# Storing groups 5 and 6 in partition-strided pieces, some of them from GpSimd

## The chip, the cores and the metric

The kernel runs on one core of one Trainium2 chip. The metric is the device time of the core in microseconds, the median of repeated executions: 132.0 us before the change (3 runs, 132.0 to 132.01).

## The reference

A batched matrix product of 32 pairs, in float32:

```python
# x: (32, 256, 512)   y: (32, 512, 384)   result: (32, 256, 384)
np.einsum('bij,bjk->bik', x, y).astype(np.float32)
```

The inputs are 16.8 MB and 25.2 MB, the output 12.6 MB. The kernel rounds the inputs to float16 for TensorE and accumulates in float32.

## The kernel before

The 32 products are done in N = 8 groups of Q = 4. A group's four products fill the 128 partitions together: each product has PQ = 32 of them, so partition p belongs to product p // 32 of the group. For x a partition holds R = 8 rows of i (a run of 16 KB in memory), for y T = 16 rows of j (24 KB), for the output 8 rows of i (12 KB).

SyncE issues all DMAs. Groups 0 and 1 are loaded at once (L75), the later ones each when the buffer of two groups earlier has been rounded (L98 to L102). GpSimd rounds x and y to float16 (L126, L136), VectorE transposes x in blocks of 32x32 (L156), TensorE multiplies four products at a time, each on 32 rows of its array (L217), into eight PSUM banks: four for the half e = 0 of the output rows, four for e = 1. ScalarE and VectorE copy the banks into `o_sb` (L165), which holds the output of all eight groups. TensorE starts a half only when the copies of the half before last have been made (`take(s_act)`, `take(s_dve)`), and it increments `s_pe` as it finishes chunks and banks; so the value of `s_pe` that says that chunk 0 of the last half of a group is done also says that all groups before that one are in `o_sb`.

The output leaves in three stores, all by `store(first, last)` (L93), each a DMA over 128 partitions:

- groups 0 to 4 (`JOINED` = 5) when TensorE has done chunk 0 of the last half of group 5 (L103, L104);
- groups 5 and 6 when it has done chunk 0 of the last half of group 7 (L105, L106). A partition gives two runs of 12 KB, one for each group;
- group 7 when the last copies have been made (L107 to L109).

All DMAs of SyncE stand in one queue, in the order of issue. After the last issue SyncE tells GpSimd through `s_sp` (L110) and waits until the three stores have landed (L111; each landing adds 16 to `s_out`). GpSimd, when its casts are done, waits for `s_sp` and clears the kernel's semaphores (L144, L145).

Of the kernel before, what the change touches and what calls it, by code (L numbers as in the profile page):

```python
# [10 lines left out]
P = 128  # L11
Q = 4
NE = 2
STEP = 4
STRAIGHT = 2
JOINED = 5
# [3 lines left out]
def kernel(  # L20
# [6 lines left out]
    nc = tc.nc  # L27
# [4 lines left out]
    PQ = P // Q  # L32
    R = I // PQ
# [3 lines left out]
    N = B // Q  # L37
    NC = T // STEP

    def sbuf(name, shape, dtype):  # L40
        return nc.alloc_sbuf_tensor(name, shape, dtype).ap()
# [3 lines left out]
    o_sb = sbuf("o_sb", [P, N, NE, H, K], F32)  # L45
# [6 lines left out]
    s_x = [nc.alloc_semaphore(f"s_x{n}") for n in range(N)]  # L52
    s_y = [nc.alloc_semaphore(f"s_y{n}") for n in range(N)]
    s_xt = nc.alloc_semaphore("s_xt")
    s_yr = nc.alloc_semaphore("s_yr")
    s_cast = nc.alloc_semaphore("s_cast")
    s_free = nc.alloc_semaphore("s_free")
    s_act = nc.alloc_semaphore("s_act")
    s_dve = nc.alloc_semaphore("s_dve")
    s_pe = nc.alloc_semaphore("s_pe")  # L60
    s_sp = nc.alloc_semaphore("s_sp")
    s_out = nc.alloc_semaphore("s_out")
    mine = s_x + s_y + [s_xt, s_yr, s_cast, s_free, s_act, s_dve, s_pe, s_sp]
    nums = sorted(s.num for s in mine)
    assert nums == list(range(nums[0], nums[-1] + 1)) and s_out.num == nums[-1] + 1

# [21 lines left out]
    def chunk_done(n, e, a):  # L88
        return (n * NE + e) * MARKS + (a + 1 if a < NC - 1 else MARKS)

    sp = nc.sync

    def store(first, last):  # L93
        groups = out[first * Q : last * Q].rearrange("(n g) (s f) k -> (g s) n f k", g=Q, s=PQ)
        src = o_sb[:, first:last].rearrange("p n e h k -> p n (e h) k")
        sp.dma_start(out=groups, in_=src).then_inc(s_out, 16)

    for n in range(2, N):  # L98
# [3 lines left out]
        load_y(n)  # L102
    sp.wait_ge(s_pe, chunk_done(JOINED, NE - 1, 0))  # L103
    store(0, JOINED)  # L104
    sp.wait_ge(s_pe, chunk_done(N - 1, NE - 1, 0))  # L105
    store(JOINED, N - 1)  # L106
    sp.wait_ge(s_act, NE)  # L107
    sp.wait_ge(s_dve, NE)
    store(N - 1, N)  # L109
    sp.sem_inc(s_sp, 1)  # L110
    sp.wait_op(s_out, 16 * 3, "sem-ge").then_inc(s_out, -16 * 3)  # L111

    def pieces(n):
        w = 1 if n in (0, N - 2, N - 1) else 2
        return [(a, a + w) for a in range(0, NC, w)]

    po = nc.gpsimd

    def round_x(n):
        po.wait_ge(s_x[n], 16)
        for e in range(NE):
            if n:
                po.wait_ge(s_free, max(2 * n - 2 + e, 1))
            po.tensor_copy(  # L126
                x_r[:, e], x_sb[n % 2][:, e * H : (e + 1) * H]
            ).then_inc(s_cast, 1)

    def round_y(n):  # L130
        po.wait_ge(s_y[n], 16)
        for a, b in pieces(n):
            if n:
                po.wait_ge(s_pe, chunk_done(n - 1, NE - 1, b - 1))
            s = slice(a * STEP, b * STEP)
            ins = po.tensor_copy(y_r[:, s], y_sb[n % 2][:, s])  # L136
            ins.then_inc(s_yr, b - a if b < NC else b - a + NC)
# [3 lines left out]
    for n in range(1, N):  # L141
        round_x(n)
        round_y(n)
    po.wait_ge(s_sp, 1)  # L144
    po.sem_clear(range(nums[0], nums[-1] + 1))  # L145

# [84 lines left out]
    with te.Fori(0, N):  # L231
        with te.Fori(0, NE) as e:
            take(s_act)
            take(s_dve)
            for t in range(T):
# [3 lines left out]
                for g in range(Q):  # L239
                    s = slice(g * PQ, (g + 1) * PQ)  # L240
# [40 lines left out]
```

## Time and profile before

| | |
|---|---|
| median of 3 runs | 132.0 us |
| the profiled execution | 132.13 us |
| its span, first to last instruction | 130.8 us |
| granted TensorE clock, mean | 0.823 |
| bytes read from HBM, written to it | 41.94 MB, 12.58 MB |

The transfers, by what is issued, with the size of one and the median time from its issue to its landing:

```profile
## 6 DMA issues: line engine op xcount, KB each, us to landing
y_sb<-in_y_dram SPq DMA_DIRECT2D x8, 3072.0 KB, 16.8
x_sb<-in_x_dram SPq DMA_DIRECT2D x8, 2048.0 KB, 17.0
out_dram<-o_sb SPq DMA_DIRECT2D x1, 7680.0 KB, 33.9
out_dram<-o_sb SPq DMA_DIRECT2D x1, 3072.0 KB, 17.3
out_dram<-o_sb SPq DMA_DIRECT2D x1, 1536.0 KB, 11.5
```

How to read it: a core has 16 DMA engines, and a DMA is done by several of them, each with its own packets; a transfer that is issued while others are still queued lands long after its issue. PE is TensorE's matmul, PEld its weight load, DVE VectorE, ACT ScalarE, POOL GpSimd, SP SyncE; a "q" behind a name is the engine's sequencer. Rows of stretches give the stretch, its length, busy time and count for PE, PEld, DVE, ACT and POOL, the granted clock, the busy share of the DMA engines and their GB/s, where a packet is counted in the stretch in which it starts. Rows of waits give who waited for whom, the sum in us, how often, and the longest.

### The profile page before, as it was taken

To read this page: it belongs to the slowest core of one execution; us is meant where nothing else is said; L and a number is where in the kernel's file an instruction comes from. 1 tells how busy PE (TensorE), PEld (TensorE's weight loads), DVE (VectorE), ACT (ScalarE), POOL (GpSimd) and SP (SyncE) were. 2 spreads that over 40 slices of the span, in tenths; PEclk is the share of its full clock that TensorE was granted. 3 is DMA by queue.
4 is the path that set the end of the run, shared out by engine and by line. 5 is a ranking of instruction groups with operands and counts; after the bars stand their busy time and mean duration, and the time that the engine had idled before them with its cause. 6 is when DMAs were issued, how large, how long until landed. Compare 5 with 4: busy or idle time off the path is not lost. (4 is left out here: it accounts for less than half of the span.)

```text
span 130.8 us, 3199 instructions
## 1 busy us (share of the span) xinstructions
PE 61.4 (47%) x1024; PEld 46.7 (36%) x1024; DVE 82.7 (63%) x144; ACT 84.1 (64%) x178; POOL 74.2 (57%) x42
## 2 busy tenths in 40 slices
PE   0000009910992589089329905980975499100000
PEld 0000009800991566046129604970953236000000
DVE  0000036899379999985997997599999957920000
ACT  0400000599659989993998899399999957994000
POOL 0006991199929965992899459758973970000000
PEclk9999999995589689977986985599599959965555
DMA  5999999999999999999999999999999999999995
GB/s 120 451 396 441 421 431 451 443 408 428 451 413 421 438 443 401 436 436 443 423 458 398 443 408 466 398 418 436 463 398 408 427 438 425 436 428 421 425 440 248
DMA packets 3379, 54.55 MB, mean 417 GB/s; under 512 B 304, under 2 KB 304, under 8 KB 304
## 3 DMA queue, kind: packets, MB, share of 16 engines
q1 hardware_dynamic: 3376, 54.53, 98.1%
q14 instruction: 3, 0.02, 0.0%
HBM read 41.94 MB, written 12.58 MB: 417 GB/s over the span
## 5 line engine op out<-in xcount | busy, mean ns | idle before, releaser
L165 ACT COPY o_sb<-o_ps (+1 forms) x176 | 82.6, 469 | 31.7 <-PE o_ps L217 29.6
L217 PE MATMUL o_ps<-y_r,xt_sb 32*128 32x384 f16 x1024 | 61.4, 384 | 50.4 <-PEq L214 49.5
L217 PEld LDWEIGHTS o_ps<-y_r,xt_sb 32*128 32x128 f16 x1024 | 46.7, 107 | 64.6 <-issue 56.8
L156 DVE STREAM_TRANSPOSE xt_sb<-x_r 128x256 f32<-128x256 f32 x64 | 38.1, 626 | 30.9 <-POOL x_r L126 18.4
L136 POOL CAST y_r<-y_sb 128x1536 f16<-128x1536 f32 (+1 forms) x22 | 44.3, 2049 | 15.8 <-DMA y_sb<-in_y_dram 15.3
L165 DVE COPY o_sb<-o_ps 32x384 f32 (+1 forms) x80 | 44.6, 557 | 1.6
L126 POOL CAST x_r<-x_sb 128x2048 f16<-128x2048 f32 x16 | 30.2, 1893 | 16.8 <-DVE o_sb L165 12.1
L202 ACT ACT_TABLE_LOAD x1 | 1.3, 1283 | 3.4 <-PEq L78 3.4
L265 POOL MEMSET const-float32-0.0<- 128x1 f32 x1 | 0.1, 98 | 0.2 <-issue 0.2
L202 ACT COPY spare<-const-float32-0.0 1x1 f32<-1x1 f32 x1 | 0.2, 190 | 0.0
L265 POOL MEMSET const-bfloat16-1.0<- 128x1 bf16 x1 | 0.1, 101 | 0.0
L265 POOL MEMSET const-uint8-127<- 128x1 uint8 x1 | 0.1, 101 | 0.0
L265 POOL MEMSET const-float32-1.0<- 128x1 f32 x1 | 0.1, 98 | 0.0
## 6 DMA issues: line engine op xcount, KB each, us to landing
y_sb<-in_y_dram SPq DMA_DIRECT2D x8, 3072.0 KB, 16.8
x_sb<-in_x_dram SPq DMA_DIRECT2D x8, 2048.0 KB, 17.0
out_dram<-o_sb SPq DMA_DIRECT2D x1, 7680.0 KB, 33.9
out_dram<-o_sb SPq DMA_DIRECT2D x1, 3072.0 KB, 17.3
out_dram<-o_sb SPq DMA_DIRECT2D x1, 1536.0 KB, 11.5
```

What stands on the lines that cost most here:

```text
L126: po.tensor_copy(x_r[:, e], x_sb[n % 2][:, e * H : (e + 1) * H]).then_inc(s_cast, 1)
L136: ins = po.tensor_copy(y_r[:, s], y_sb[n % 2][:, s])
L156: v.transpose(xt_w[:, w], words[:, e, w]).then_inc(s_xt, 1)
L165: ins = copy(o_sb[g * PQ : (g + 1) * PQ, n, e, h], o_ps[h * PQ : (h + 1) * PQ, e * Q + g, :K],)
L202: a_.copy(spare, nc.const_aps.tensor(0.0, [1, 1], F32))
L217: return te.add_instruction(mybir.InstMatmult(name=nc.get_next_instruction_name(), start_tensor_calc=start, stop_tensor_calc=stop, tile_si ...
L265: nc = _bacc.Bacc("TRN2", target_bir_lowering=False, num_devices=1)
```

## The change

The store of groups 5 and 6 is replaced by seven DMAs. A new function `store_rows(eng, sem, first, step, rows, f0, f1)` stores, for both groups, the output rows f0 to f1 (of the 8) of the partitions first, first + step and so on. SyncE stores the even partitions (64), then 1, 5, 9, ... (32), then 3, 11, 19, ... (16). Of the remaining 16 partitions, 7, 15, ..., 127, it stores rows 1 to 7 (10.5 KB in each group) of the first four in one DMA and of the fifth, 39, in another. GpSimd stores row 0 (1.5 KB in each group) of these five, and then all 8 rows of the other eleven, 47 to 127, after the same mark of TensorE and its last casts. GpSimd's two DMAs count on a semaphore of their own, `s_few`, for which SyncE waits after it has issued the last store and before it tells GpSimd to clear the semaphores. `s_out` now counts seven DMAs of SyncE: groups 0 to 4, these five, and group 7.

```diff
+    s_few = nc.alloc_semaphore("s_few")
...
+    def store_rows(eng, sem, first, step, rows, f0=0, f1=R):
+        dst = out[JOINED * Q : (N - 1) * Q].rearrange("(n g) (s f) k -> (g s) n f k", g=Q, s=PQ)
+        src = o_sb[:, JOINED : N - 1].rearrange("p n e h k -> p n (e h) k")
+        p = slice(first, first + (rows - 1) * step + 1, step)
+        eng.dma_start(out=dst[p, :, f0:f1], in_=src[p, :, f0:f1]).then_inc(sem, 16)
...
     sp.wait_ge(s_pe, chunk_done(N - 1, NE - 1, 0))
-    store(JOINED, N - 1)
+    store_rows(sp, s_out, 0, 2, P // 2)
+    store_rows(sp, s_out, 1, 4, P // 4)
+    store_rows(sp, s_out, 3, 8, P // 8)
+    store_rows(sp, s_out, 7, 8, 4, 1)
+    store_rows(sp, s_out, 39, 8, 1, 1)
     sp.wait_ge(s_act, NE)
     sp.wait_ge(s_dve, NE)
     store(N - 1, N)
+    sp.wait_ge(s_few, 16 * 2)
     sp.sem_inc(s_sp, 1)
-    sp.wait_op(s_out, 16 * 3, "sem-ge").then_inc(s_out, -16 * 3)
+    sp.wait_op(s_out, 16 * 7, "sem-ge").then_inc(s_out, -16 * 7)
...
+    po.wait_ge(s_pe, chunk_done(N - 1, NE - 1, 0))
+    store_rows(po, s_few, 7, 8, 5, 0, 1)
+    store_rows(po, s_few, 47, 8, 11)
     po.wait_ge(s_sp, 1)
     po.sem_clear(range(nums[0], nums[-1] + 1))
```

More of the change, by code (lines that the diff above doesn't have):

```diff
@@ L61 @@
     s_sp = nc.alloc_semaphore("s_sp")
+    s_few = nc.alloc_semaphore("s_few")
     s_out = nc.alloc_semaphore("s_out")
-    mine = s_x + s_y + [s_xt, s_yr, s_cast, s_free, s_act, s_dve, s_pe, s_sp]
+    mine = s_x + s_y + [s_xt, s_yr, s_cast, s_free, s_act, s_dve, s_pe, s_sp, s_few]
     nums = sorted(s.num for s in mine)
```

## The prediction

> **What bounds the kernel now.** I read the page first, for the busy shares, then the work by stretches of time, then what SyncE's queue waited for, and last the transfers in the final microseconds, since those decide how much there is to win.
>
> ```profile
> span 130.8 us, 3199 instructions
> PE 61.4 (47%) x1024; PEld 46.7 (36%) x1024; DVE 82.7 (63%) x144; ACT 84.1 (64%) x178; POOL 74.2 (57%) x42
> DMA packets 3379, 54.55 MB, mean 417 GB/s; under 512 B 304, under 2 KB 304, under 8 KB 304
> q1 hardware_dynamic: 3376, 54.53, 98.1%
> ```
>
> No compute engine is busy for two thirds of the span; the 16 DMA engines are busy for 98.1% of it, with one queue. The chain of waits is no help: it ends at the last copy, as it follows instructions and not transfers. The stretches show it better.
>
> ```profile
> 0.00:1.70 1.70, 0.00 (x0) 0.00 (x0) 0.00 (x0) 0.00 (x0) 0.20 (x4) 1.00 0.00 0
> ...
> 106.00:119.40 13.40, 5.74 (x96) 3.04 (x95) 7.15 (x13) 10.77 (x23) 1.03 (x1) 0.75 1.01 431
> 119.40:126.30 6.90, 0.00 (x0) 0.00 (x0) 0.00 (x0) 0.00 (x0) 0.00 (x0) 0.50 1.01 433
> 126.30:128.90 2.60, 0.00 (x0) 0.00 (x0) 0.00 (x0) 0.00 (x0) 0.00 (x0) 0.50 0.98 421
> ```
>
> After the start-up of 1.7 us the engines never run dry, and from 119.4 us on nothing computes: the kernel ends when its bytes are out. At 433 GB/s one of 16 engines moves 27.06 KB (of 1,000 bytes) per us; I use that below. So an edit of the last stores can pay in one way only: by spreading the same bytes over the engines so that the last one ends sooner. How unevenly they end now is seen in the completions. The 304 packets under 512 B on the page are 16 for each of the 19 DMAs: each engine closes its part of a DMA with one, so such packets count the engines that finish the last store.
>
> In 129.0 to 129.6 us, then 129.6 to 130.0, then 130.0 to 130.8:
>
> ```profile
> DMA packets 22, 0.16 MB, mean 266 GB/s; under 512 B 9, under 2 KB 9, under 8 KB 9
> ...
> DMA packets 7, 0.01 MB, mean 31 GB/s; under 512 B 6, under 2 KB 6, under 8 KB 6
> ...
> DMA packets 1, 0.00 MB, mean 0 GB/s; under 512 B 1, under 2 KB 1, under 8 KB 1
> ```
>
> Nine engines finish before 129.6, six more before 130.0, one alone after that. The median engine is near 129.55. To place the late one:
>
> ```profile
> 129.25:129.50 0.25, 0.00 (x0) 0.00 (x0) 0.00 (x0) 0.00 (x0) 0.00 (x0) 0.50 0.82 344
> 129.50:129.80 0.30, 0.00 (x0) 0.00 (x0) 0.00 (x0) 0.00 (x0) 0.00 (x0) 0.50 0.01 0
> 129.80:130.20 0.40, 0.00 (x0) 0.00 (x0) 0.00 (x0) 0.00 (x0) 0.00 (x0) 0.50 0.08 31
> ```
>
> A packet is counted where it starts: 31 GB/s over 0.40 us is 12.4 KB, one packet of 12,288 B, begun after 129.80 when the other 15 engines had begun their last before 129.50. It takes 12,288 / 27.06 KB = 0.45 us, so the late engine ends at 130.25 or later; I take 130.3. The next ends before 129.95 (begun by 129.50, plus 0.45). The late engine alone thus costs about 0.35 us. That is the prize, 0.27% of the time.
>
> **The change, part by part.** It takes the store of groups 5 and 6 apart.
>
> ```profile
> SPq L96 <- PE o_ps L217: 23.5, 1, 23.5
> SPq L111 <- SPq L111: 11.1, 1, 11.1
> SPq L108 <- DVE o_sb L165: 5.0, 1, 5.0
> SPq L96 <- ACT o_sb L165: 4.0, 1, 4.0
> ...
> 109.82 9.80 SPq L96 DMA_DIRECT2D out_dram<-o_sb  x2
> ...
> 101.33 5.70 POOL L136 CAST y_r<-y_sb 128x1536 f16<-128x1536 f32 x4 [2.18 <-DMA y_sb<-in_y_dram]
> ...
> L96 SPq DMA_DIRECT2D out_dram<-o_sb x3: 345/390/403, 85.9 to 119.3; - x3
> ...
> DMA to landing us min/median/max: 11.5/17.3/33.9
> L145 POOLq EVENT_SEMAPHORE_RANGE_CLEAR  x1: 163/163/163, 119.7 to 119.7; - x1
> ```
>
> *Issue on SyncE.* One issue at 109.82 becomes five, at 0.345 to 0.403 us each: up to 4 x 0.40 = 1.6 us more, done by about 111.8. Behind them stand only the waits for the last copies (5.0 and 4.0 us) and the last store, issued at 119.3: 7 us to spare. The engines meanwhile work on the store of groups 0 to 4 (issued at 85.9, landed 33.9 us later, at 119.8). Cost nothing; without that cover, 1.6 us.
>
> *Issue on GpSimd.* It finishes its casts at 101.33 + 5.70 = 107.03, waits for the same mark of TensorE and issues two DMAs. No row shows a DMA issued by GpSimd. The bounds: 0.35 us each as on SyncE below; above, its idle time to the end, 130.8 - 109.8 = 21 us, for the two together. Its transfers go ahead in the 20 us in which other packets fill the engines. I take nothing, as even ten times SyncE's issue (2 x 4 us) ends at 118. If the cover were gone, the largest row, 24,576 B, would take 0.91 us at the end.
>
> *The new wait.* SyncE waits for GpSimd's transfers after the last store is issued. Behind it stand the increment of s_sp and the final wait; for s_sp only GpSimd's clear of the semaphores waits (0.163 us, at 119.7 now). Nothing as long as GpSimd's rows land before about 130.6, at most 0.2 us beyond.
>
> *The bytes.* The total stays. In the old store each engine had 3,072 KB / 16 = 196,608 B. Of the new ones the three sets of 64, 32 and 16 rows divide by 16: 172,032 B to each engine. The remaining 16 rows come in portions: SyncE sends 4 of 21,504 B and 1 of 21,504 B, GpSimd 5 of 3,072 B and 11 of 24,576 B. If every row of a DMA falls to an engine of its own and GpSimd's five and eleven fall to different ones, eleven engines get 24,576 B and four 21,504 + 3,072 = 24,576 B, all as before. The fifth row's large part is a DMA by itself: nothing puts it on the engine that has that row's small part. So one engine is lighter by 21,504 B, 0.79 us, and one is heavier by that, or two by 0.40 us each. The trace names no engine of a packet, so whether the lighter one is the late one isn't shown.
>
> [...]
>
> *Smaller packets.* All packets but the 304 of 4 bytes are over 8 KB now. New are pieces of 10,752 B and ten of 1,536 B, and 4 x 16 + 2 x 16 completions in place of 16. Between 0 and 0.1 us on an engine; I take 0.05, as the 4-byte ones vanish in the shares above.
>
> **Sum.** If the lighter engine is the late one, it ends at 130.3 - 0.79 = 129.5; a heavier one of the middle ends at 129.55 + 0.40 = 129.95, as do the next-latest now. The end moves from 130.3 to 129.95, and with 0.05 for small packets by -0.30 us. The profiled execution took 132.13 us, 1.33 more than its span, and 0.13 more than the median of 132.0. So 132.13 - 0.30 = 131.83 there, and 131.7 against the median. The bounds: -0.4 to 0 if one engine took all 0.79 (129.55 + 0.79 = 130.34).
>
> **Rivals.**
>
> *No effect.* The lighter engine is one of the middle. The late one stays at 130.3 and the heavier ones end at 129.95 to 130.34: 132.0. For it: only 1 engine of 16 is the late one. Against it: nothing in the rows.
>
> *Uneven portions.* The heavier engine is the late one (130.3 + 0.40 to 0.79, so 132.4 to 132.8), or GpSimd's eleven rows fall on the engines that already hold the four: then the first has 46,080 B too much, 1.70 us, and ends at 129.55 + 1.70 = 131.25: 132.9. For it: eleven and five rows don't divide by 16, and the trace has no such DMA. It decides as soon as one engine gets over 24 KB too much.
>
> [...]
>
> [...]
>
> **How the numbers follow.** Forecast (late engine relieved) 0.36, at 131.7, own range 131.5 to 131.95. No effect 0.18, 132.0. Uneven portions 0.24, 132.4 to 132.9. Colliding rows 0.22, 133 to 138. [...] What tells from no change here is about 0.2%, 0.26 us: faster 0.36, same 0.18, slower 0.46. The first three cases hold 0.78 up to 132.9, and the light end of the collisions brings 0.8: 131.4 (gain of 0.4 and rounding) to 134.0.
>
> **What would show it.** Right: the last store's completions closer together, none alone after 130.0, rate in the store of groups 5 and 6 still about 430 GB/s. No effect: the same lone completion at 130.3. Uneven: a completion 0.4 us or more after the others, with the rate unchanged until 129. [...] GpSimd's landing after 130 would prove the cover of its issue wrong.

## The result, and the profile after

The changed kernel takes 133.41 us (median of 5 runs, 133.34 to 133.69) beside 132.0 us of the kernel before on the same chip: a ratio of 1.0111, with a 95% interval of 1.0096 to 1.0126. It is slower by about 1.4 us, where a gain of 0.3 us was forecast. The profiled execution took 133.69 us.

The page of the changed kernel, its head and its DMA queues:

```profile
span 132.3 us, 3205 instructions
...
DMA packets 3475, 54.55 MB, mean 412 GB/s; under 512 B 395, under 2 KB 395, under 8 KB 400
...
q1 hardware_dynamic: 3392, 54.24, 96.9%
q0 software_dynamic: 80, 0.29, 0.5%
```

GpSimd's DMAs have a queue of their own, q0, with 0.29 MB. The bytes are the same 54.55 MB, so the loss is in how long the engines need for them. The changed kernel by stretches, from the end of the computation on:

```profile
119.40:126.30 6.90, 0.00 (x0) 0.00 (x0) 0.00 (x0) 0.00 (x0) 0.00 (x0) 0.50 1.01 422
126.30:128.90 2.60, 0.00 (x0) 0.00 (x0) 0.00 (x0) 0.00 (x0) 0.00 (x0) 0.50 0.97 386
128.90:129.50 0.60, 0.00 (x0) 0.00 (x0) 0.00 (x0) 0.00 (x0) 0.00 (x0) 0.50 0.96 410
129.50:130.00 0.50, 0.00 (x0) 0.00 (x0) 0.00 (x0) 0.00 (x0) 0.00 (x0) 0.50 0.70 295
130.00:130.50 0.50, 0.00 (x0) 0.00 (x0) 0.00 (x0) 0.00 (x0) 0.00 (x0) 0.50 0.35 148
130.50:131.00 0.50, 0.00 (x0) 0.00 (x0) 0.00 (x0) 0.00 (x0) 0.00 (x0) 0.50 0.17 74
131.00:131.50 0.50, 0.00 (x0) 0.00 (x0) 0.00 (x0) 0.00 (x0) 0.00 (x0) 0.50 0.17 74
```

Read the share and the rate together. Between 126.3 and 128.9 us the engines are busy for 0.97 of the time, as before (0.98), but move 386 GB/s in place of 421: a packet takes longer. Then they do not end together: the rate falls in steps until 131.5 (a packet is counted where it starts; the last one ends at 131.96). The completions in 129.5 to 130.2, 130.2 to 131.0 and 131.0 to 132.3 us:

```profile
DMA packets 24, 0.18 MB, mean 264 GB/s; under 512 B 9, under 2 KB 9, under 8 KB 9
...
DMA packets 10, 0.07 MB, mean 92 GB/s; under 512 B 4, under 2 KB 4, under 8 KB 4
...
DMA packets 6, 0.04 MB, mean 28 GB/s; under 512 B 3, under 2 KB 3, under 8 KB 3
```

Nine engines, then four, then three. Before, 15 finished within 0.7 us and one stood 0.38 us apart (0.35 by the prediction's reading); now seven are late, up to 2.3 us behind the first.

The trace names no engine of a packet, but it has the start and the duration of each, and in both traces a packet mostly starts within some 10 ns of the end of another. Taken as the next one of the same engine, the engines of the changed kernel can be followed one by one. A packet of 12,288 B takes 0.460 us in the median of both traces. The engine that ends last, at 131.96, had no short DMA of SyncE; its two packets of the set of 16 took 1.24 and 1.16 us, 1.47 us more than usual. The three next-latest ends (130.81, 131.19, 131.85) also have long packets in that set, 0.40 to 0.79 us more than usual, and the one at 131.85 lost another 0.79 us in its two pieces of the four short rows. The two engines that had row 39 as well, the heavier ones, end at 130.06 and 130.47, and none of their packets is long.

The issues of the changed kernel (least, median and longest ns of one, first and last start), and the time from GpSimd's issue to its landing:

```profile
L100 SPq DMA_DIRECT2D out_dram<-o_sb x5: 663/696/775, 110.2 to 113.2; - x5
...
L100 POOL DMA_DIRECT2D out_dram<-o_sb x2: 557/626/696, 110.4 to 111.1; - x2
...
DMA to landing us min/median/max: 5.7/6.5/7.3
```

All is issued by 114 us, and GpSimd's rows have landed by 111.1 + 7.3 = 118.4, over 13 us before the last packet ends.

One part of the difference between the two spans isn't the change's. In 32.4 to 36.0 us the loads ran at 382 GB/s in this execution, at 437 in the one before (first row):

```profile
32.40:36.00 3.60, 3.58 (x45) 3.42 (x49) 1.48 (x3) 2.35 (x5) 3.60 (x2) 0.50 1.02 437
...
32.40:36.00 3.60, 2.30 (x27) 1.97 (x31) 1.95 (x5) 3.44 (x8) 3.60 (x3) 0.50 0.92 382
```

That is 55 GB/s x 3.6 us = 198 KB, or 0.46 us, in a place that the change does not touch; some of it is made up, and by 86 us the engines are 0.15 MB behind (35.84 in place of 35.99), about 0.35 us. This execution is the slowest of the five, 0.28 us over their median; the ratios below rest on all runs of a kernel.

### The profile page after: what moved, and what is told of

Same layout as the page of the kernel before. It is cut to its first block, busy times and chain, and to the rows that moved or that the text cites. A ratio compares the mean times of both kernels' runs of the same rounds, so it can differ in the third digit from the quotient of the medians.

```text
span 132.3 us, 3205 instructions
## 1 busy us (share of the span) xinstructions
PE 63.7 (48%) x1024; PEld 49.0 (37%) x1024; DVE 82.5 (62%) x144; ACT 84.1 (64%) x178; POOL 75.3 (57%) x44
## 2 busy tenths in 40 slices
DMA packets 3475, 54.55 MB, mean 412 GB/s; under 512 B 395, under 2 KB 395, under 8 KB 400
## 3 DMA queue, kind: packets, MB, share of 16 engines
q1 hardware_dynamic: 3392, 54.24, 96.9%
## 5 line engine op out<-in xcount | busy, mean ns | idle before, releaser
L235 PE MATMUL o_ps<-y_r,xt_sb 32*128 32x384 f16 x1024 | 63.7, 392 | 48.4 <-PEq L232 48.3
L235 PEld LDWEIGHTS o_ps<-y_r,xt_sb 32*128 32x128 f16 x1024 | 49.0, 110 | 62.7 <-issue 55.0
L150 POOL CAST y_r<-y_sb 128x1536 f16<-128x1536 f32 (+1 forms) x22 | 44.3, 2048 | 14.4 <-DMA y_sb<-in_y_dram 14.4
L100 POOL DMA_DIRECT2D out_dram<-o_sb x2 | 1.2, 626 | 3.1 <-PE o_ps L235 3.1
```

Of the source, the lines that this page charges most:

```text
L100: eng.dma_start(out=dst[p, :, f0:f1], in_=src[p, :, f0:f1]).then_inc(sem, 16)
L235: return te.add_instruction(mybir.InstMatmult(name=nc.get_next_instruction_name(), start_tensor_calc=start, stop_tensor_calc=stop, tile_si ...
```

## The experiments

Each ratio is to the kernel before, run on the same chip, with its 95% interval. All kernels change the store of groups 5 and 6 alone.

Two theories stood first. Either the portions are uneven (too many bytes on some engines), or rows that are read in small strided sets get in each other's way. GpSimd's queue was a third suspect.

**Strided sets without GpSimd and without short DMAs**

```diff
-    store_rows(sp, s_out, 7, 8, 4, 1)
-    store_rows(sp, s_out, 39, 8, 1, 1)
+    store_rows(sp, s_out, 7, 8, P // 8)
...
-    store_rows(po, s_few, 7, 8, 5, 0, 1)
-    store_rows(po, s_few, 47, 8, 11)
```

> SyncE stores groups 5 and 6 alone, in four strided sets of 64, 32, 16 and 16 partitions; no short DMA and nothing from GpSimd. Uneven portions (two engines carry 10,752 B more, and the short DMAs are to blame): 132.0 us as before, and no packet of the last stores much slower than the others. Colliding rows (strided sets as such are slow beside the last store): 132.7 to 133.4, the rate between 125 and 128 us stays near 384 GB/s. GpSimd's transfers to blame: 132.0.

132.39 us, 1.0027 [1.0016, 1.0039]: slower, but by a quarter of the loss. Both "as before" theories miss, and so does the lower end for colliding rows.

**GpSimd stores whole rows, evenly**

```diff
-    store_rows(sp, s_out, 7, 8, 4, 1)
-    store_rows(sp, s_out, 39, 8, 1, 1)
...
-    store_rows(po, s_few, 7, 8, 5, 0, 1)
+    store_rows(po, s_few, 7, 8, 5)
```

> GpSimd stores all 16 remaining rows whole, five and then eleven; SyncE only the sets of 64, 32 and 16. Uneven portions: 132.0 us, as every engine has 24,576 B of them if the two DMAs fall on different engines; 132.9 or more if both start on the same engine. Colliding rows: 132.7 or more. GpSimd's transfers to blame: 133 or more, as in the changed kernel.

133.36 us, 1.0096 [1.0079, 1.0113]: the full loss with no uneven DMA of SyncE. It seemed to point to GpSimd. The trace of this kernel shows the same pattern as in the changed kernel: the two engines that end last (131.71 and 131.76) had long packets in the set of 16, 1.57 and 1.39 us more than usual over the two of each.

**Row 39 by GpSimd too**

```diff
-    store_rows(sp, s_out, 39, 8, 1, 1)
...
-    store_rows(po, s_few, 7, 8, 5, 0, 1)
-    store_rows(po, s_few, 47, 8, 11)
+    store_rows(po, s_few, 7, 8, 4, 0, 1)
+    store_rows(po, s_few, 39, 8, 12)
```

> As the changed kernel, but GpSimd stores row 39 whole too (four pieces of 1.5 KB, then twelve whole rows), so that no engine is heavier by the count of bytes; the DMA of four rows by SyncE stays. Uneven portions by bytes alone: 132.0 to 132.3 us, no lone pair of late engines. Colliding rows, or the DMA of four rows to blame: 132.7 to 133.4, as the changed kernel.

133.73 us, 1.0118 [1.0101, 1.0135]: the portion that made an engine heavier is gone and nothing is won.

**The short DMAs and small sets first**

```diff
-    store_rows(sp, s_out, 0, 2, P // 2)
-    store_rows(sp, s_out, 1, 4, P // 4)
-    store_rows(sp, s_out, 3, 8, P // 8)
-    store_rows(sp, s_out, 7, 8, 4, 1)
-    store_rows(sp, s_out, 39, 8, 1, 1)
+    store_rows(sp, s_out, 39, 8, 1, 1)
+    store_rows(sp, s_out, 7, 8, 4, 1)
+    store_rows(sp, s_out, 3, 8, P // 8)
+    store_rows(sp, s_out, 1, 4, P // 4)
+    store_rows(sp, s_out, 0, 2, P // 2)
```

> As the changed kernel, with SyncE's five DMAs of groups 5 and 6 in the opposite order: 1 row, 4 rows, 16, 32, 64. Uneven portions: the same bytes per engine, so the same 133.4 us within 0.2. Colliding at the border between the last set and the last store: the set of 64 now stands there, and the lowered rate of 125 to 128 us is gone or moves to 119 to 121 us, where the short DMAs now stand; 132.4 to 133.4.

133.3 us, 1.0092 [1.0075, 1.0109]. The time fits both theories, the place only one. This kernel's transfers in 119.0 to 122.8 us, then in 124.6 to 128.4:

```profile
DMA packets 160, 1.43 MB, mean 376 GB/s; under 512 B 43, under 2 KB 43, under 8 KB 43
...
DMA packets 149, 1.63 MB, mean 430 GB/s; under 512 B 16, under 2 KB 16, under 8 KB 16
```

The low rate (376 GB/s) has moved to where the small sets now stand, and the set of 64 that now borders on the last store runs at full rate (430 GB/s). So the loss sits with the sets of few rows, not with the border to the last store as such.

**Sets of 32 only**

```diff
-    store_rows(sp, s_out, 0, 2, P // 2)
-    store_rows(sp, s_out, 1, 4, P // 4)
-    store_rows(sp, s_out, 3, 8, P // 8)
-    store_rows(sp, s_out, 7, 8, P // 8)
+    for q in range(4):
+        store_rows(sp, s_out, q, 4, P // 4)
```

(This diff and that of the next kernel are against the first experiment.)

> SyncE alone stores groups 5 and 6 as four strided sets of 32 partitions. If the stretched packets come only with DMAs of one row for each engine (the sets of 16), there are none here and the time is 132.0 us within 0.2. If strided sets, or more DMAs as such, cost something, it is 132.3 us or more, as with the sets of 64, 32, 16 and 16 (132.39).

132.1 us, 1.0004 [0.9988, 1.002]: no loss.

**The two sets of 16 apart**

```diff
     store_rows(sp, s_out, 0, 2, P // 2)
-    store_rows(sp, s_out, 1, 4, P // 4)
     store_rows(sp, s_out, 3, 8, P // 8)
+    store_rows(sp, s_out, 1, 4, P // 4)
     store_rows(sp, s_out, 7, 8, P // 8)
```

> The sets of 64, 32, 16 and 16 by SyncE alone, but the two sets of 16 no longer follow each other: 64, 16, 32, 16. If a set of 16 is stretched at its borders to other sets, there are now four such borders in place of two (between the two sets of 16 there was one without harm): 132.8 to 133.4 us, as much as with GpSimd. If GpSimd's transfers made the 133.4 us, it stays at 132.4.

133.11 us, 1.0104 [1.0071, 1.0138]: most of the loss or all of it (1.1 us by the medians; single runs from 132.68 to 133.88), from a change of order alone, without GpSimd.

**Group 6 by GpSimd, over all 128 partitions** (`store` takes the engine and the semaphore as arguments here)

```diff
-    store_rows(sp, s_out, 0, 2, P // 2)
...
-    store_rows(sp, s_out, 39, 8, 1, 1)
+    store(JOINED, JOINED + 1)
...
-    store_rows(po, s_few, 7, 8, 5, 0, 1)
-    store_rows(po, s_few, 47, 8, 11)
+    store(JOINED + 1, N - 1, po, s_few)
```

> SyncE stores group 5 and GpSimd group 6, each one DMA over all 128 partitions: the most bytes through GpSimd's queue, no strided sets. If GpSimd's queue itself is to blame for the loss: 133 us or more. If only the sets of few rows are: 132.0 us within 0.3, no stretched packets.

131.97 us, 1.0 [0.9987, 1.0013]. The page has q0 with five times the bytes of the changed kernel, and nothing is lost: GpSimd's queue as such is cleared.

```profile
q0 software_dynamic: 144, 1.57, 2.8%
```

A row of transfers with its share gives the mean time of a packet: share x 16 engines x length of the stretch, divided by the packets without the completions. The same 3.8 us, 124.6 to 128.4, in the kernel before:

```profile
DMA packets 146, 1.60 MB, mean 420 GB/s; under 512 B 16, under 2 KB 16, under 8 KB 16
...
q1 hardware_dynamic: 146, 1.60, 98.6%
```

0.986 x 60.8 / 130 = 0.46 us. In the changed kernel:

```profile
DMA packets 163, 1.53 MB, mean 403 GB/s; under 512 B 37, under 2 KB 37, under 8 KB 37
...
q1 hardware_dynamic: 163, 1.53, 103.0%
```

62.6 / 126 = 0.50 us, although some packets are smaller now. With the sets of 16 apart:

```profile
DMA packets 147, 1.43 MB, mean 375 GB/s; under 512 B 31, under 2 KB 31, under 8 KB 31
...
q1 hardware_dynamic: 147, 1.43, 100.1%
```

60.9 / 116 = 0.52 us. With the sets of 32:

```profile
DMA packets 155, 1.66 MB, mean 437 GB/s; under 512 B 20, under 2 KB 20, under 8 KB 20
...
q1 hardware_dynamic: 155, 1.66, 102.4%
```

62.3 / 135 = 0.46 us. The packets of 12,288 B are the same, and a mean hides how few of them are long: from 118 us on, 12 of the 404 in the changed kernel took over 5% more than 0.460 us, the longest 1.24, and 29 of 396 with the sets of 16 apart, the longest 1.32. In the kernel before, with the sets of 32 and with group 6 by GpSimd, one of some 400 did in each, the longest 0.504 us.

**Eight sets of 16, two ways.** What in a set of 16 costs? First neighbouring partitions, then every eighth (in place of all strided sets and of GpSimd's stores):

```diff
+    for q in range(8):
+        store_rows(sp, s_out, 16 * q, 1, 16)
```

> SyncE alone stores groups 5 and 6 as eight sets of 16 partitions that follow each other (0 to 15, 16 to 31, ...). [...] If it is the number of completions, or one row for each engine, that costs: 16 rows in place of 112 in such DMAs' neighbourhood, 132.5 to 134 us.

143.79 us, 1.0912 [1.088, 1.0944]. The 196,608 B of an engine, 7.27 us at the full rate, take 11.8 us more: 0.38 of the rate. That is far above the 132.5 to 134 us that were expected if the completions, or one row for each engine, made the cost.

```diff
+    for q in range(8):
+        store_rows(sp, s_out, q, 8, P // 8)
```

> SyncE alone stores groups 5 and 6 as eight sets of 16 partitions with a step of 8 (0, 8, ..., 120; then 1, 9, ...). [...] If every set of 16 costs by itself as each of the two did: 135 us or more.

138.32 us, 1.048 [1.0463, 1.0498]. In 120 to 124 us of this kernel:

```profile
DMA packets 106, 0.88 MB, mean 221 GB/s; under 512 B 34, under 2 KB 34, under 8 KB 34
...
q1 hardware_dynamic: 106, 0.88, 103.3%
```

1.033 x 64 / 72 = 0.92 us for a packet: twice 0.46, with the engines busy all the time. But a set of 16 has also two packets to a completion (72 to 34 here) where a set of 32 has four (140 to 36 in 120 to 124 us). The next experiment separates that.

**Eight sets of 32, one group at a time** (`store_rows` gets the groups, n0 to n1, as further arguments)

```diff
+    for q in range(4):
+        for n in range(2):
+            store_rows(sp, s_out, q, 4, P // 4, n0=n, n1=n + 1)
```

> SyncE alone stores groups 5 and 6 as eight sets of 32 partitions (step 4, one group at a time). As many DMAs, packets and completions for each engine as the eight sets of 16 (138.3 us), two packets to a completion, but two partitions for each engine in place of one. If it is the partitions that collide: 132.0 us within 0.3, packets of 0.46 us. If it is the completions, two packets apart, or the many short DMAs: about 138 us.

132.12 us, 1.0004 [0.9995, 1.0014]. In 120 to 124 us:

```profile
DMA packets 214, 1.73 MB, mean 433 GB/s; under 512 B 73, under 2 KB 73, under 8 KB 73
...
q1 hardware_dynamic: 214, 1.73, 102.5%
```

1.025 x 64 / 141 = 0.465 us. As many DMAs, packets and completions as with the eight sets of 16, at twice the rate. So what is left is the partitions of a DMA: 32 with a step of 4 ran at 433 GB/s, 16 with a step of 8 at 221. In what way they cost isn't shown: each partition has its own rows of the output, in every run, so a delay of the reads in SBUF isn't told from one of the writes in memory.

**Does a lighter engine pay at all?** Whole rows stay in DMAs over 128 partitions; only the 1.5 KB of row 0 are dealt out unevenly, and as a control evenly.

```diff
+    store_rows(sp, s_out, 0, 1, P, 1)
+    for first in range(5, 37, 4):
+        store_rows(sp, s_out, first, 1, 4, 0, 1)
+    store_rows(sp, s_out, 37, 1, 3, 0, 1)
...
+    store_rows(po, s_few, 0, 1, 5, 0, 1)
+    store_rows(po, s_few, 40, 1, 88, 0, 1)
```

> Rows 1 to 7 of all partitions of groups 5 and 6 go in one DMA of SyncE over 128 partitions (each engine on its own partitions); the 1.5 KB of row 0 go so that four engines get 24,576 B, the fifth 3,072 B and eleven 24,576 B (eight DMAs of 4 partitions and one of 3 by SyncE, 5 and 88 partitions by GpSimd). The same lighter engine as in the changed kernel, without whole rows in DMAs of few rows. If that engine is the late one and only it, as the forecast had it: 131.7 us, faster by 0.2 to 0.4. If it is not the late one in runs without a profile: 132.0. If many pieces of 1.5 KB cost by themselves, or get in the way of others: 132.2 to 133.

132.74 us, 1.0059 [1.0036, 1.0083]; single runs from 132.22 to 133.82.

```diff
+    store_rows(sp, s_out, 0, 1, P, 1)
...
+    store_rows(po, s_few, 0, 1, P, 0, 1)
```

> The same, but GpSimd stores the 1.5 KB of row 0 of all 128 partitions in one DMA, evenly. Tells what the small pieces cost: 132.0 to 132.1 us if nothing, 132.3 or more if small pieces are slow.

132.05 us, 1.0003 [0.9994, 1.0012]. Dealt out evenly, the small pieces cost nothing here (131.97 before). Dealt out unevenly they cost 0.8 us. Completions of the uneven kernel in 130.4 to 130.6 and in 130.6 to 131.7 us:

```profile
DMA packets 2, 0.01 MB, mean 61 GB/s; under 512 B 1, under 2 KB 1, under 8 KB 1
...
DMA packets 2, 0.01 MB, mean 11 GB/s; under 512 B 1, under 2 KB 1, under 8 KB 1
```

One engine ends alone, and later than the late one of the kernel before. In this run, making one engine lighter made another one late; followed through the trace, that engine left SyncE's short DMAs 0.8 us after all others (127.68, beside 126.87), and packets of 1,536 B took up to 0.77 us, where most take 0.065. Which of the nine short DMAs does it wasn't tried.

No version beat the kernel before.

## Why the prediction was wrong

**What bounds the kernel: right.** The last transfers set the end: the last packet ends at 130.31 of 130.8 us before, at 131.96 of 132.3 in the changed kernel. The four even splits without sets of 16 (two with sets of 32, group 6 by GpSimd, row 0 by GpSimd) give 132.0 to 132.1 us.

**Issue on SyncE and GpSimd: right in effect, wrong in size.** The issues took 0.66 to 0.78 us each on SyncE, not up to 0.40, and 0.56 to 0.70 on GpSimd; the cover held, as all of them were done by 114 us, and the last store was still issued at 119.1.

**The new wait: right.** GpSimd's rows landed by 118.4 us, and SyncE's wait for them cost nothing.

**The bytes: the step that failed.** The sum counted bytes on engines, and took it that a row costs the same in any DMA. The count itself seems sound. SyncE's queue q1 has 3,392 packets, of which 3,050 carry data (2,048 of loads, 640 + 128 of the 128-partition stores, 224 of the three sets, 10 of the short DMAs); the 342 completions left are 16 for each of 21 DMAs, and 6 for the two short ones. So four rows went to four engines and one row of two groups to two, and the heavier engines had 10,752 B more, 0.40 us each, as the sum had it. But those two ended at 130.06 and 130.47, not last, and evening the portions out (row 39 by GpSimd, or all 16 rows by GpSimd) won nothing. What failed is that the sum gave every row its 0.91 us (two packets of 0.45) in whatever DMA it stood: in the set of 16 the two packets of the engine that ended last took 2.39 us. The sum had no term for that; only the 0.22 of the colliding rows allowed for it.

**Smaller packets: next to nothing, as forecast.** With small pieces dealt evenly the time is 132.05 us. The count was off: 395 - 304 = 91 packets under 512 B were added, 107 in place of 16, and no packet of 1,536 B shows in the changed kernel; GpSimd's ten pieces went as five packets of 3,072 B.

**Colliding rows: the right rival, too low.** I gave it 0.22, at 133 to 138 us. No run shows those 1 to 6 us as a term. In their place the runs showed 132.39 to 133.73 us with one or two sets of 16 among larger sets, 138.32 and 143.79 us with eight. The rate fell, to 422 and then 386 GB/s, with the engines busy for 1.01 and 0.97 of the time. But the set of 64 runs at the full rate (430 GB/s in the second row of the kernel with the short DMAs first), and so do the sets of 32 (437 GB/s). The long packets are those of the sets of 16 and of the short DMAs, one row for each engine, and a few of the stores beside them; while GpSimd's rows, one for each engine too, went out, the rate was as before (431 GB/s in 110.0 to 118.5 us, 432 before). What made it decide is the spread: a few packets on a few engines are delayed (12 of 404), and the end waits for the last one. So 133.41 us lies at the light end of this rival, for which the range had been widened to 134.0. Eight sets of every eighth partition cost 6.3 us; 196,608 B for each engine at half the rate would make 7.27. Sets of 16 neighbours cost 11.8 us, and their 143.79 us are beyond the rival's upper end.

**The late engine relieved: open.** The ends of the changed kernel are so spread that its relief can't be seen, and the one kernel made to test it got another late engine. Nothing shows that a lighter engine pays.

**Order matters, and why isn't shown.** Two sets of 16 next to each other cost 0.3% (132.39 us), the same two apart 1.0% (133.11). In the changed kernel GpSimd took most of the rows that would have stood next to the set of 16, and in the kernel where it stores whole rows all of them: 1.1% and 1.0%. Packets took up to 1.24 us in the changed kernel, 2.7 times 0.46, and 1.32 with the sets apart, not twice as with eight sets of 16. The runs show the effect of the order, not its cause.

## What to carry to other kernels

Equal bytes weren't equal time here: with groups 5 and 6 stored in sets of 32 partitions the kernel took 132.1 us, in sets of 16 with a step of 8 it took 138.3. So look not only at the bytes for each engine, but also at which partitions stand in one DMA. The sign of it was a share of busy DMA engines that stayed near 1 (0.97, 0.98 before) while the rate fell (386 GB/s, 421 before). Before a store is cut into sets of partitions to move bytes between engines, time the cut with equal portions. Here the cut cost 1.4 us, and the last engine's lateness of 0.38 us was all that it could have given back.

## What the runs showed of the hardware that was not expected

- Stores of 64 and 32 partitions with a step of 2 and 4 ran at the rate of 128 (420 to 433 GB/s before): 430 and 437 GB/s, 0.46 us for 12,288 B. 16 partitions with a step of 8 ran at half of it when eight such sets followed each other: 221 GB/s, 0.92 us. In the changed kernel, with one set of 16, each of the four engines that ended last had a packet of 0.86 to 1.24 us in that set.
- GpSimd's queue carried 1.57 MB beside SyncE's with no loss (131.97 us). In the changed kernel its rows overtook those that SyncE's queue held: they landed at 118.4 us at the latest, while SyncE's strided sets, issued at the same time, were still being written after 119.
- The issue of a strided set or a short DMA on SyncE took 0.66 to 0.78 us in the changed kernel, that of a store over 128 partitions 0.35 to 0.41. It isn't fixed: the eight sets of 32 were issued within 7.78 us and the store behind them in 0.36, the eight sets of 16 with a step of 8 within 10.35 us and the store behind them in 2.46.
